# Two batches of 64x64 products on all quarters of the array, softmax denominators inverted by ln and exp on ACT, and other choices of the planner in a two-layer hybrid decoder trunk

## The chip, the core and the metric

The kernel runs on one core of one Trainium2 chip. The core has a matrix engine (PE, which takes weights by separate load instructions, PEld), a vector engine (DVE), an activation engine (ACT), a general engine (POOL), and a queue on SP that issues the DMAs. The metric is the device time of one execution in microseconds (us); lower is better. Beside the timed runs there is one profiled execution, whose records are the trace.

## The reference

Two layers run one after the other on `x` of 512 positions by 1024 channels, float32. Cut to what matters here:

```
for l in range(2):
    h = rmsnorm(x, norm_g[l]);  p = h @ w_in[l]          # one wide projection, split by columns
    o_a = causal latent attention, 8 heads, gated by silu
    o_b = causal attention with a forget gate, 8 heads of 64, gated by silu
    o_c = RWKV-7, 8 heads of 64, gated by silu:
          S_t = S_{t-1} diag(w_t) - (S_{t-1} kk_t)(kk_t a_t)^T + v_t k_t^T ;  y_t = S_t r_t
    merged = sigmoid(g_a)*(o_a @ w_pa) + sigmoid(g_b)*(o_b @ w_pb) + sigmoid(g_c)*(o_c @ w_pc)
    x = x + merged @ w_out
```

Both attentions are softmaxes over 512 keys: `p @ v` is divided by the row sums of `p`. The RWKV recurrence over 512 steps is what the change rewrites most.

## The kernel before, in words

Everything lies transposed: channels on the 128 partitions, the 512 positions along the free dimension. A projection (`proj`, line 776) makes 128 output channels with eight steps over the 1024 inputs, each of three matmuls of 128x128 weights by 512 columns (`mm3`, lines 769 to 772): weights and inputs are split into a high and a low part, and high times high, high times low and low times high are added in one PSUM bank (tag `acc`, three banks). The weights arrive by DMA as float32 (`raw`), 256 columns at a time; `copy` (line 638, on ACT or DVE) makes the high part and `combine` (line 650, on DVE or POOL) the low part, into a ring of six buffers `w`.

The RWKV branch goes by pairs of heads (four pairs in a layer, eight in all); one head lies on partitions 0 to 63, the other on 64 to 127. The 512 steps are cut in 8 chunks of 64. `rwkv_inv` (line 950) makes for each chunk and head a product of 128x128 from 64 rows (line 974, tile names `KB`, `KR`; results in the banks `xk` for the first head, `ch` for the second), masks it into `At`, and inverts a unit triangular matrix: 32x32 blocks on POOL (lines 996, 998), the rest by 32x32 products (lines 1016 and 1022), the inverse in `W`. `rwkv_chain` (line 1027) then makes seven batches of products, each of 16 (8 chunks by 2 heads) and each into the one bank `ch`, by the helper `each` (line 1056): the transposes `KT` as products with the identity (`ch<-cs,KR`), `R` (`ch<-KV,At`), `M` (`ch<-KR,W`), the update of `VSA` (`ch<-At,W`), `Q` (`ch<-At`), `G` (`ch<-KV`, 128 rows by 64) and the transition of the state (`ch<-KV,At` again). All but `G` are 64x64 products in full float32, which the chip runs as two passes each, so a batch of 16 shows as 32 instructions. Both heads of such a batch lie on two quarters of the array, on a diagonal. Each batch needs the batch before it, copied out of PSUM (`copy`). Six steps of the state (lines 1095, 1096) and the output products (lines 1102, 1106) follow.

An attention pair ends in `finish` (line 1230): `dn`, the row sums, is inverted by DVE's reciprocal (line 1232), multiplied by the gate `sg` and then by `ot`. There are 16 of these, one for a pair of heads in each of two attentions and two layers.

The order of the instructions is not the order of the code. Five streams (RWKV preparation, RWKV chain, attention, merge gates, merge) are recorded together, and `plan` (line 214) sets the order on each engine by a list scheduler: of the instructions that could start, the one with the longest way to the end goes first (`urgency`), by a table of costs (`_cost`). For copies, fills and sums it also picks the engine: `elsewhere` (line 349) leaves an instruction to another engine where that one would be done earlier. On PE it may prefer an instruction of the present tile shape (lines 389 to 392), and a change of tile shape costs it a drain (`DRAIN`, lines 426 to 428). A pair of instructions can be tied by hand with `order` (line 580), which puts the one ahead of the other without a wait.

Of the kernel before, what the change touches and what calls it, by code (L numbers as in the profile page):

```python
# [134 lines left out]
PORT_WAIT = 1500  # L135
LN_WAIT = 3000
# [77 lines left out]
def plan(insts, tags, manual, flex, margin, replay=None):  # L214
# [17 lines left out]
    for inst in insts:  # L232
        k = len(ops)
        op = Op(inst, k, box)
        op.cost = _cost(op, psum)
        op.cross = []
        op.array = array(op) if op.kind == "InstMatmult" else None
        op.port = {}
# [15 lines left out]
        op.after.pop(k, None)  # L254
    for a, b in manual:
        ops[index[a]].after[index[b]] = False
# [41 lines left out]
    def forward(follow=None):  # L298
# [13 lines left out]
        mode, pe_end, last_start = (128, 128), 0.0, 0.0  # L312
        other = lambda k: ops[k].func in {"exp": ("Ln",), "ln": ("Exp", "Tanh")}[table]

        def due(k, e):

            return max([ready[k]] + [end[a] + lat(ops[a], ops[k]) for a in ops[k].cross if ops[a].lane != e])

        def ok(k):
            return not wait[k] and not need[k]  # L320

        def release(k):
            if ok(k):
                for e, _ in ops[k].costs:
                    heapq.heappush(later[e], (due(k, e), k))
# [23 lines left out]
        def elsewhere(k, e):  # L349

            mine = starts(k, e) + dict(ops[k].costs)[e]
            for x, cost in ops[k].costs:
                if x != e:
                    ahead = sum(dict(ops[j].costs)[x] for u, j in avail[x]
                                if u < -ops[k].urgency and not taken[j] and len(ops[j].costs) == 1)
                    if max(starts(k, x), free[x] + ahead) + cost < mine:
                        return True
            return False

        def choose():  # L360
# [9 lines left out]
            for s, e in soon:  # L370
# [18 lines left out]
                if e == PE and ops[pick[1]].array != mode:  # L389
# [17 lines left out]
        for _ in ops:  # L407
# [14 lines left out]
            if op.kind == "InstMatmult":  # L422
                c0, c1 = op.outs[0][1:3]
# [107 lines left out]
def build(tc, x_t, wpk, wsm, wv, vec, cst, out, order_of=None, pick={}, queues=None, margin=2.0):  # L531
# [48 lines left out]
    def order(later, earlier):  # L580
        no_sync(later.ins, earlier.ins, "psum bank order")
        manual.append((later.ins.name, earlier.ins.name))

# [132 lines left out]
    for l in range(L):  # L716
# [233 lines left out]
        def rwkv_inv(p, front, v):  # L950
# [3 lines left out]
            KR = rpool.tile([128, 8, 2, 64], F32, name="KR", tag="KR", bufs=2)  # L954
            dve.scalar_tensor_tensor(KR[:, :, 0, :], c64(kn), -1024.0, c64(lw), op0=ALU.mult, op1=ALU.mult)
            combine(KR[:, :, 1, :], c64(r), c64(cum), ALU.mult)
# [45 lines left out]
            for h in range(2):  # L1002
                for b in range(2):
                    o_, l_ = 64 * h + 32 * b, 16 * b + 8 * h
# [5 lines left out]
            half_ = [[slice(o_, o_ + 32) for o_ in (64 * h, 64 * h + 32, SA[h])] for h in range(2)]  # L1010
            for h, (r1, r2, s1) in enumerate(half_):
                fill(W[r2, :, 0:32], 0.0)
                dve.transpose(X[s1], W[r1, :, 0:32])
            for c in range(8):
                for h, (r1, r2, s1) in enumerate(half_):
                    pe.matmul(ps[r2, 0, c, :], At[s1, h, c, 32:64], X[s1, c, :], start=True, stop=True)
            for h, (r1, r2, s1) in enumerate(half_):
                copy(X[r2], ps[r2, 0])
            yield
            for c in range(8):  # L1020
                for h, (r1, r2, s1) in enumerate(half_):
                    pe.matmul(ps[r1, 1, c, :], X[r2, c, :], W[r2, c, 32:64], start=True, stop=True)
            for h, (r1, r2, s1) in enumerate(half_):
# [3 lines left out]
        def rwkv_chain(p, ops):  # L1027
# [19 lines left out]

            R = G = At[:, 0, :, 0:64]
            M = At[:, 1, :, 0:64]
            KT, Q = KR[:, :, 0, :], KR[:, :, 1, :]  # L1050
            chunks = lambda: PS("ch").rearrange("p (c t) -> p c t", t=64)

            def each(ps, out, lhs, rhs):
                for c in range(8):
                    for h, hs in enumerate(HS):
                        pe.matmul(ps[out(h), c, :], lhs(h, c), rhs(h, c), start=True, stop=True)  # L1056

            same, swap = (lambda h: HS[h]), (lambda h: HS[1 - h])
            ps = chunks()
            each(ps, same, lambda h, c: KR[HS[h], c, 0, :], lambda h, c: C["ident"][HS[h], HS[h]])  # L1060
            copy(KT, ps)
            yield
            ps = chunks()
            each(ps, same, lambda h, c: At[HS[h], h, c, 0:64], lambda h, c: VSA[HS[h], c, HS[h]])
            copy(R, ps)
            yield
            ps = chunks()
            each(ps, swap, lambda h, c: W[HS[h], c, :], lambda h, c: KT[HS[h], c, :])
            copy(M, ps)
            yield  # L1070
            ps = chunks()
            each(ps, swap, lambda h, c: W[HS[h], c, :], lambda h, c: R[HS[h], c, :])
            for h, hs in enumerate(HS):
                copy(VSA[HS[1 - h], :, hs], ps[HS[1 - h]])
            yield
            ps = chunks()
            each(ps, same, lambda h, c: M[HS[1 - h], c, :], lambda h, c: At[HS[1 - h], h, c, 64:128])
            dve.tensor_tensor(Q, ps, Q, op=ALU.add)
            yield
            ps = chunks()  # L1080
            each(ps, same, lambda h, c: KBn[:, c, HS[h]], lambda h, c: VSA[:, c, HS[h]])
            dve.tensor_tensor(G, ps, lam.unsqueeze(2).broadcast_to([128, 8, 64]), op=ALU.mult)
            yield
            ps = chunks()
            each(ps, same, lambda h, c: M[HS[1 - h], c, :], lambda h, c: KBn[HS[1 - h], c, HS[h]])
            for h, hs in enumerate(HS):
                fill(KBn[hs, :, HS[1 - h]], 0.0)
                dve.tensor_tensor(KBn[hs, :, hs], ps[hs], C["ident"][hs, hs].unsqueeze(1).broadcast_to([64, 8, 64]),
                                  op=ALU.add)
            yield  # L1090
            Sh = rpool.tile([128, 8, 64], F32, name="Sh", tag="Sh", bufs=1)
            state = [None, G[:, 0, :]] + [Sh[:, c, :] for c in range(2, 8)]
# [137 lines left out]
        def finish(A):  # L1230
            dn, ot = A["dn"], A["ot"]
            dve.reciprocal(dn, dn)  # L1232
# [515 lines left out]
```

## Time and profile before

| | us |
|---|---|
| three timed runs, median (lowest, highest) | 1417.71 (1416.28, 1420.82) |
| the profiled execution, its own time | 1415.31 |
| its span, first to last instruction | 1413.5 |
| PE busy | 1367.5 (97%) |
| PE weight loads busy | 1085.1 (77%) |
| DVE busy | 1171.3 (83%) |
| ACT busy | 777.3 (55%) |
| POOL busy | 452.8 (32%) |

Busy time of an engine is the time in which at least one of its instructions is recorded as running. Matmuls overlap: the record of one goes on while the next has begun, so what a matmul costs PE is read from start to start of two neighbours and not from its duration. The granted clock of PE is 0.995 of its full 2.4 GHz over the whole execution.

### The profile page before, as it was taken

Reading aid. Unit: us, or ns where it says so; the run is one execution under the profiler, and the core shown is the slowest. Engines: PE = TensorE matmul, PEld = TensorE weight load, DVE = VectorE, ACT = ScalarE, POOL = GpSimd, SP = SyncE. Lnnn points to the kernel's source line nnn. Section 1 sums busy time; section 2 is a strip of 40 time slices with the busy share of each in tenths; the row PEclk is TensorE's granted clock in tenths of the full one; section 3 lists DMA queues with packets and bytes.
Section 4 is the critical chain, followed back from the end, with each engine's and each line's share of the span. In section 5 each row is a group of like instructions: output and inputs, shape, how many; then the busy total and the mean of one; then the engine's idle time right before and its main releaser. Section 6 shows DMA issues by size and latency. Waiting matters only on the chain. (4 is left out here: it accounts for less than half of the span.)

```text
span 1413.5 us, 25288 instructions
## 1 busy us (share of the span) xinstructions
PE 1367.5 (97%) x8756; PEld 1085.1 (77%) x8756; DVE 1171.3 (83%) x2653; ACT 777.3 (55%) x1539; POOL 452.8 (32%) x875
## 2 busy tenths in 40 slices
PE   7799999999999999999999999999999999999998
PEld 5676877877778887878877777777876778787787
DVE  8867878888987879878788789789789978898784
ACT  6545637565775466442355656484576664764320
POOL 2152373542650212221002453633724711022210
PEclk9999999999999999999999999999999999999999
DMA  5342322232243234455534342232323233434563
GB/s 170 104 126 75 103 79 87 68 85 81 73 119 95 86 109 159 141 171 169 179 112 139 102 114 82 61 85 84 87 76 116 72 95 90 139 130 156 174 200 97
DMA packets 114625, 158.70 MB, mean 112 GB/s; under 512 B 36544, under 2 KB 44608, under 8 KB 114496
## 3 DMA queue, kind: packets, MB, share of 16 engines
q1 hardware_dynamic: 114496, 157.08, 36.8%
q8 instruction: 69, 1.13, 0.3%
q14 instruction: 60, 0.49, 0.1%
HBM read 128.72 MB, written 28.31 MB: 111 GB/s over the span
## 5 line engine op out<-in xcount | busy, mean ns | idle before, releaser
L770 PE MATMUL acc<-hh,w 128*128 128x512 f32 x1008 | 371.0, 405 | 15.6 <-DVE hh L638 5.1
L650 POOL TENSOR_TENSOR w<-raw,w 128x256 fp32r<-128x256 f32 (+1 forms) x215 | 180.4, 845 | 626.9 <-DVE w L638 292.1
L772 PE MATMUL acc<-hh,w 128*128 128x512 f32 x1008 | 369.8, 404 | 5.3 <-DVE w L650 5.1
L771 PE MATMUL acc<-hl,w 128*128 128x512 f32 x1008 | 366.8, 402 | 1.1 <-DVE hl L650 0.9
L638 ACT ACTIVATE w<-raw 128x256 fp32r<-128x256 f32 (+1 forms) x367 | 147.4, 413 | 247.6 <-PE acc L772 137.9
L770 PEld LDWEIGHTS acc<-hh,w 128*128 128x128 f32 x1008 | 188.7, 190 | 59.9 <-ACT w L638 6.3
L772 PEld LDWEIGHTS acc<-hh,w 128*128 128x128 f32 x1008 | 189.6, 190 | 45.1 <-DVE w L650 5.6
L771 PEld LDWEIGHTS acc<-hl,w 128*128 128x128 f32 x1008 | 189.3, 189 | 41.6 <-DVE hl L650 3.0
L650 DVE TENSOR_TENSOR w<-raw,w 128x256 fp32r<-128x256 f32 x485 | 207.7, 441 | 8.0 <-ACT w L638 3.3
L638 DVE CAST w<-raw 128x256 fp32r<-128x256 f32 (+1 forms) x333 | 98.6, 304 | 98.8 <-PE acc L772 78.6
L996 POOL TENSOR_TENSOR W<-W,NL 128x60 f32<-128x60 f32 (+24 forms) x248 | 88.1, 355 | 72.6 <-DMA NL<-d 55.4
L1204 PE MATMUL wk<-qk 96*128 96x512 f32 (+7 forms) x320 | 99.1, 324 | 1.0 <-ACT vt L638 0.6
L998 POOL TENSOR_TENSOR W<-W 128x60 f32<-128x60 f32 (+24 forms) x248 | 87.9, 354 | 16.9
L650 DVE TENSOR_TENSOR PP<-wk,PP 128x512 fp32r<-128x512 f32 (+3 forms) x128 | 61.4, 485 | 16.5 <-ACT PP L638 14.8
L1204 PEld LDWEIGHTS wk<-qk 128*128 128x128 f32 (+2 forms) x320 | 59.6, 189 | 13.7 <-DVE PP L650 2.1
L1179 DVE CUSTOM_DVE_ANT_0 wk<-wk,cmask 128x128 f32<-128x128 f32 (+3 forms) x128 | 61.3, 497 | 2.5 <-PE wk L1178 1.7
L638 ACT ACTIVATE PP<-wk 128x512 fp32r<-128x512 f32 (+3 forms) x93 | 39.8, 435 | 28.5 <-PE av L1218 24.8
L1232 DVE RECIPROCAL do<-do 128x512 f32<-128x512 f32 x16 | 53.5, 3345 | 0.1
L1205 DVE TENSOR_TENSOR wk<-wk,dmask 128x128 f32<-128x128 f32 x128 | 37.2, 293 | 18.7 <-PE wk L1204 17.9
L1209 ACT ACTIVATE wk<-wk,ncum 128x512 f32<-128x512 f32 (+1 forms) x64 | 31.5, 492 | 27.6 <-DVE wk L1205 27.5
L1178 PE MATMUL wk<-qk 96*128 96x384 f32 (+7 forms) x128 | 42.2, 340 | 2.5 <-DVE ty L1179 2.1
L1216 PE MATMUL av<-PP,Vh 128*128 128x512 f32 (+3 forms) x128 | 42.3, 330 | 0.5 <-ACT do L638 0.2
(529 smaller groups left out, 2894.9 us busy)
## 6 DMA issues: line engine op xcount, KB each, us to landing
raw<-wpk SPq DMA_DIRECT2D x326, 256.0 KB, 2.7
tx<-thd SPq DMA_DIRECT2D x54, 256.0 KB, 3.5
thd<-zth SPq DMA_DIRECT2D x48, 256.0 KB, 2.0
tx<-odr SPq DMA_DIRECT2D x22, 256.0 KB, 3.0
raw<-wpk SPq DMA_DIRECT2D x32, 128.0 KB, 2.4
NL<-d SPq DMA_DIRECT2D x32, 128.0 KB, 2.7
odr<-sg SPq DMA_DIRECT2D x14, 256.0 KB, 2.3
x<-x_t SPq DMA_DIRECT2D x8, 256.0 KB, 4.2
```

What stands on the lines that cost most here:

```text
L638: lambda q: act.activation(dst, src, AF.Copy) if q == ACT else dve.tensor_copy(dst, src))
L650: any_of(costs, lambda q: (dve if q == DVE else gp).tensor_tensor(dst, a, b, op=op))
L770: pe.matmul(ps, wh, xh, start=first, stop=False)
L771: pe.matmul(ps, wh, xl, start=False, stop=False)
L772: pe.matmul(ps, wl, xh, start=False, stop=last)
L996: gp.tensor_tensor(tv, WL[:, 0:m, s:s + 1].broadcast_to([128, m, n]), NL[:, s:s + 1, s + 1:32].broadcast_to([128, m, n]), op=ALU.mult)
L998: gp.tensor_tensor(WL[:, 0:m, s + 1:32], WL[:, 0:m, s + 1:32], tv, op=ALU.add)
L1178: pe.matmul(ps[:, 0:n], t[sr, A["sq"], 128 * i:n], t[sr, 2, 0:n], start=True, stop=True)
L1179: dve.tensor_tensor_reduce(out=ps[:, 0:n], in0=ps[:, 0:n], in1=cmask[:, 512 - n:512], scale=1.0, scalar=NEG, op0=ALU.add, op1=ALU.max, acc ...
L1204: pe.matmul(pv, t[rows, k, js], t[rows, q, q0:512], start=i == 0, stop=i == len(passes) - 1)
L1216: pe.matmul(av[:, q0:512], vh, ph, start=j == 0, stop=False)
L1232: dve.reciprocal(dn, dn)
```

## The change

The diff has five parts.

- `rwkv_chain`: the transposes `KT` become four 128x128 transposes in place of 16 products with the identity, and four copies of 64x256 put them on the other head's partitions. `R` and `M` become one batch of 32 products, in two banks (`ch` and `xk`), and the update of `VSA` and the transition of the state another; in each, the four products of a chunk lie on the four quarters of the array. `Q` and `G` stay batches of 16. For this the inverse `W` lies with the heads exchanged (`SA`), `KR` has its two halves one after the other, and the states go into `KT` in place of a tile of their own.
- `beside` ties the products of a batch one behind the other by `order`, in the two batches and in the product of line 974, where the two heads then alternate.
- The planner starts two batches that are tied together only when both of their banks are free (`mate`), and goes on with a batch that it has begun as long as one of its products can run (`burst`). That holds for every product on a part of the array.
- `PRICE = 400`: where DVE or ACT could take an instruction and POOL could not, DVE is counted as 400 ns later than by its cost.
- `finish`: DVE's reciprocal is replaced by two ACT instructions, ln and exp of minus that.

```diff
+PRICE = 400
...
     for a, b in manual:
-        ops[index[a]].after[index[b]] = False
+        a, b = index[a], index[b]
+        ops[a].after[b] = False
+        if a in firsts and b in firsts:
+            mate[b], mate_of[a], joint[firsts[a]] = a, b, firsts[b]
+    for op in ops:
+        if op.array and op.array != (128, 128):
+            n = op.outs[0][0]
+            op.burst = joint.get(n, n)
...
-            mine = starts(k, e) + dict(ops[k].costs)[e]
+            mine = starts(k, e) + dict(ops[k].costs)[e] + PRICE * (e == DVE and ops[k].costs[0][0] != POOL and ops[k].costs[1][0] != POOL)
...
+                if e == PE and burst:
+                    same = min((x for x in avail[e] if not taken[x[1]] and ops[x[1]].burst == burst), default=None)
+                if same:
+                    pick = same
...
-                for c in range(4 * g, 4 * g + 4):
-                    for h, hs in enumerate(HS):
-                        pe.matmul(two[h][:, c % 4, :], KB0[hs, c].rearrange("p a t -> p (a t)"),
-                                  KR[hs, c].rearrange("p a t -> p (a t)"), start=True, stop=True)
+                beside([pe.matmul(two[h][:, c % 4, :].rearrange("p (a t) -> p a t", a=2),
+                                  KB0[hs, c].rearrange("p a t -> p (a t)"), KR[hs, :, c, :], start=True, stop=True)
+                        for c in range(4 * g, 4 * g + 4) for h, hs in enumerate(HS)])
...
+            for c in range(4):
+                pe.transpose(ps[:, c, :], KT[:, 2 * c:2 * c + 2, :].rearrange("p c t -> p (c t)"), C["ident"])
+            for i, es in enumerate(HS):
+                for h, hs in enumerate(HS):
+                    copy(KT[SH[h], i:8:2, :], ps[es, :, hs])
+            yield
+            pr, pm = chunks(), chunks("xk")
+            beside([one(*a) for c in range(8) for h in range(2) for a in
+                    ((pr[SH[h], c, :], At[HS[h], h, c, 0:64], VSA[HS[h], c, HS[h]]),
+                     (pm[SH[h], c, :], W[SH[h], c, :], KT[SH[h], c, :]))])
+            copy(R, pr)
+            copy(M, pm)
+            yield
+            pu, pt = chunks(), chunks("xk")
+            beside([one(*a) for c in range(8) for h in range(2) for a in
+                    ((pu[SH[h], c, :], W[SH[h], c, :], R[SH[h], c, :]),
+                     (pt[HS[h], c, :], M[SH[h], c, :], KBn[SH[h], c, HS[h]]))])
...
-            dve.reciprocal(dn, dn)
+            act.activation(dn, dn, AF.Ln)
+            act.activation(dn, dn, AF.Exp, scale=-1.0)
```

On PE, the transposes `KT` of the first pair of heads. The tile `cs` holds the identity; before, each 64x64 product of the batch stands between two matmuls of a projection:

```order
L772 MATMUL wk<-w,cqh 128x192
L770 MATMUL acc<-hh,w 128x512
L1056 MATMUL ch<-cs,KR 64x64
L771 MATMUL acc<-hl,w 128x512
L1056 MATMUL ch<-cs,KR 64x64
L772 MATMUL acc<-hh,w 128x512
L1056 MATMUL ch<-cs,KR 64x64
L770 MATMUL acc<-hh,w 128x512
```

and in the changed program the same step has four transposes, of which these are the first two:

```order
L1410 MATMUL wk<-cs,kn__1233 96x128 x4
L1080 MATMUL ch<-cs,KR 128x128
L795 MATMUL acc<-hl,w 128x512
L1080 MATMUL ch<-cs,KR 128x128
L796 MATMUL acc<-hh,w 128x512
```

Transposes of the whole array have taken the place of products on a quarter. Over the program, the 128 products stand in 31 pieces before, and 32 transposes take their place.

On PE again, the batches `R` and `M` of a pair of heads. Before they are two rows of 16 products in the one bank `ch`, with other work between them:

```order
L772 MATMUL wk<-w,cqh 128x192
L1056 MATMUL ch<-KV,At 64x64 x16
L770 MATMUL wk<-w,cqh 128x192
L772 MATMUL wk<-w,ckh 128x256
L771 MATMUL wk<-w,cqh 128x192
L772 MATMUL acc<-hh,w 128x512
L772 MATMUL wk<-w,cqh 128x192
L770 MATMUL acc<-hh,w 128x512
L1056 MATMUL ch<-KR,W 64x64 x16
```

and now one stretch, in which products of the two alternate; these are the last matmul ahead of it and the first five of 32:

```order
L794 MATMUL acc<-hh,w 128x512
L1077 MATMUL ch<-KV,At 64x64
L1077 MATMUL xk<-KR,W 64x64
L1077 MATMUL ch<-KV,At 64x64
L1077 MATMUL xk<-KR,W 64x64
L1077 MATMUL ch<-KV,At 64x64
```

No other matmul stands inside any of the 16 stretches of 32.

Third, the product of line 974 on PE for the second pair of heads (in the changed program line 996). Before, the first head's products (`xk`) and the second's (`ch`) come in groups:

```order
L974 MATMUL xk<-KR,KB_1631 128x128 x3
L974 MATMUL ch<-KR,KB_1631 128x128
L974 MATMUL xk<-KR,KB_1631 128x128
L974 MATMUL ch<-KR,KB_1631 128x128 x3
L770 MATMUL wk<-w,ckh 128x256
```

and now each in turn:

```order
L795 MATMUL acc<-hl,w 128x512
L996 MATMUL xk<-KR,KB_1771 128x128
L996 MATMUL ch<-KR,KB_1771 128x128
L996 MATMUL xk<-KR,KB_1771 128x128
L996 MATMUL ch<-KR,KB_1771 128x128
L996 MATMUL xk<-KR,KB_1771 128x128
```

The eight products are the same; the neighbours now belong to different heads throughout, in 16 stretches of eight where there were 25 stretches.

## Rows read from the trace of the kernel before

**Rows 1.** The page, its busy times: us, share of the span, instructions.

```profile
PE 1367.5 (97%) x8756; PEld 1085.1 (77%) x8756; DVE 1171.3 (83%) x2653; ACT 777.3 (55%) x1539; POOL 452.8 (32%) x875
```

**Rows 2.** Waits, all engines: waiter, releaser, us in total, times, longest.

```profile
ACT w L638 <- PE acc L772: 137.9, 101, 10.7
DVE w L638 <- PE acc L772: 78.6, 86, 3.2
```

**Rows 3.** Waits of PE alone, the longest for ACT.

```profile
PE acc L770 <- ACT w L638: 4.1, 4, 1.6
```

**Rows 4.** Busy times in stretches: PE, PEld, DVE, ACT, POOL; clock; DMA.

```profile
240.00:480.00 240.00, 234.43 (x1907) 187.56 (x1907) 205.71 (x461) 153.63 (x313) 98.68 (x199) 1.00 0.30 88
```

**Rows 5.** Timeline of PE, a whole batch: start, duration, instruction, count.

```profile
231.40 0.40 PE L770 MATMUL acc<-hh,w 128*128 128x512 f32 x1
231.63 0.39 PE L772 MATMUL acc<-hh,w 128*128 128x512 f32 x1
231.95 1.15 PE L1056 MATMUL ch<-cs,KR 64*64 64x64 f32 x32
233.03 0.44 PE L1178 MATMUL wk<-qk 96*128 96x384 f32 x1
```

**Rows 6.** Timeline of PE, batch cut into single products.

```profile
120.02 0.56 PE L1056 MATMUL ch<-cs,KR 64*64 64x64 f32 x10
...
123.49 0.32 PE L1056 MATMUL ch<-cs,KR 64*64 64x64 f32 x2
...
124.17 0.32 PE L1056 MATMUL ch<-cs,KR 64*64 64x64 f32 x2
```

**Rows 7.** Timeline of PE, single transposes between matmuls.

```profile
99.88 0.27 PE L1035 MATMUL ch<-cs,KB 128*128 128x128 f32 x1
...
100.23 0.27 PE L1035 MATMUL ch<-cs,KB 128*128 128x128 f32 x1
```

**Rows 8.** Timeline of PE, batch G on 128 rows by 64 columns.

```profile
177.20 1.15 PE L1056 MATMUL ch<-KV 128*64 128x64 f32 x32
```

**Rows 9.** Timeline of PE, a batch of 32x32 products.

```profile
126.89 0.69 PE L1016 MATMUL xk<-NL,At 32*32 32x32 f32 x32
```

**Rows 10.** Timeline of PE, line 974, a stretch of both heads.

```profile
161.61 0.39 PE L771 MATMUL acc<-hl,w 128*128 128x512 f32 x1
161.93 0.93 PE L974 MATMUL xk<-KR,KB 64*128 64x128 f32 x6
...
163.87 0.38 PE L770 MATMUL wk<-w,ckh 128*128 128x256 f32 x1
```

**Rows 11.** Timeline of PE, line 974, heads in turn; then one head alone.

```profile
166.25 0.27 PE L974 MATMUL xk<-KR,KB 64*128 64x128 f32 x1
166.25 0.27 PE L974 MATMUL ch<-KR,KB 64*128 64x128 f32 x1
166.36 0.27 PE L974 MATMUL xk<-KR,KB 64*128 64x128 f32 x1
...
255.15 1.16 PE L974 MATMUL xk<-KR,KB 64*128 64x128 f32 x8
256.23 0.50 PE L772 MATMUL acc<-hh,w 128*128 128x512 f32 x1
```

**Rows 12.** Groups by line: busy us, mean ns, idle before and its releasers.

```profile
L650 DVE TENSOR_TENSOR w<-raw,w 128x256 fp32r<-128x256 f32 x485 | 207.7, 441 | 8.0 <-ACT w L638 3.3
L638 ACT ACTIVATE w<-raw 128x256 fp32r<-128x256 f32 (+1 forms) x367 | 147.4, 413 | 247.6 <-PE acc L772 137.9 <-issue 34.0 <-PE xk L772 18.0
L638 DVE CAST w<-raw 128x256 fp32r<-128x256 f32 (+1 forms) x333 | 98.6, 304 | 98.8 <-PE acc L772 78.6 <-PE xk L772 5.1 <-issue 4.8
L1232 DVE RECIPROCAL do<-do 128x512 f32<-128x512 f32 x16 | 53.5, 3345 | 0.1
L1411 ACT ACT_TABLE_LOAD x16 | 20.5, 1283 | 0.3
L1412 ACT ACTIVATE ty<-ty 128x512 f32<-128x512 f32 x16 | 10.1, 632 | 0.2
```

More of the change, by code (lines that the diff above doesn't have):

```diff
@@ L237, in plan @@
         op.array = array(op) if op.kind == "InstMatmult" else None
+        op.burst = None
         op.port = {}
@@ L311, in forward @@
         held = [(0.0, 0)] * 5
-        mode, pe_end, last_start = (128, 128), 0.0, 0.0
+        mode, pe_end, last_start, burst = (128, 128), 0.0, 0.0, None
         other = lambda k: ops[k].func in {"exp": ("Ln",), "ln": ("Exp", "Tanh")}[table]
         def due(k, e):
-            return max([ready[k]] + [end[a] + lat(ops[a], ops[k]) for a in ops[k].cross if ops[a].lane != e])
+            t = max([ready[k]] + [end[a] + lat(ops[a], ops[k]) for a in ops[k].cross if ops[a].lane != e])
+            return max(t, ready[mate[k]]) if k in mate else t
         def ok(k):
-            return not wait[k] and not need[k]
+            return not wait[k] and not need[k] and (k not in mate or wait[mate[k]] == 1 and not need[mate[k]])
         def release(k):
+            k = mate_of.get(k, k) if not taken[mate_of.get(k, k)] else k
             if ok(k):
@@ L355, in elsewhere @@
                                 if u < -ops[k].urgency and not taken[j] and len(ops[j].costs) == 1)
-                    if max(starts(k, x), free[x] + ahead) + cost < mine:
+                    if max(starts(k, x), free[x] + ahead) + cost + PRICE * (x == DVE and e == ACT) < mine:
                         return True
@@ L388, in choose @@
                         pick = same
-                if e == PE and ops[pick[1]].array != mode:
+                same = None
+                if e == PE and burst:
+                    same = min((x for x in avail[e] if not taken[x[1]] and ops[x[1]].burst == burst), default=None)
+                if same:
+                    pick = same
+                elif e == PE and ops[pick[1]].array != mode:
                     same = min((x for x in avail[e] if not taken[x[1]] and ops[x[1]].array == mode), default=None)
@@ L582, in order, with beside @@
         manual.append((later.ins.name, earlier.ins.name))
+    def beside(insts):
+        for a, b in zip(insts, insts[1:]):
+            order(b, a)
     cs = cpool.tile([128, NCST], F32, name="cs")
@@ L1049, in rwkv_chain @@
             M = At[:, 1, :, 0:64]
[L1050 to L1058, printed above, removed]
-            ps = chunks()
-            each(ps, same, lambda h, c: KR[HS[h], c, 0, :], lambda h, c: C["ident"][HS[h], HS[h]])
@@ L1061, in rwkv_chain @@
-            copy(KT, ps)
+            KT, Q = KR[:, 0], KR[:, 1]
+            SH = HS[::-1]
+            chunks = lambda tag="ch": PS(tag).rearrange("p (c t) -> p c t", t=64)
+            one = lambda *a: pe.matmul(*a, start=True, stop=True)
+            ps = PS("ch").rearrange("p (c t) -> p c t", t=128)
+            for c in range(4):
[3 more added lines that the diff above has]
+                    copy(KT[SH[h], i:8:2, :], ps[es, :, hs])
@@ new lines, in rwkv_chain @@
+            for h, hs in enumerate(HS):
+                copy(VSA[SH[h], :, hs], pu[SH[h]])
+            ps = chunks()
+            for c in range(8):
+                for hs in HS:
+                    one(ps[hs, c, :], KBn[:, c, hs], VSA[:, c, hs])
+            dve.tensor_tensor(G, ps, lam.unsqueeze(2).broadcast_to([128, 8, 64]), op=ALU.mult)
+            for h, hs in enumerate(HS):
+                fill(KBn[hs, :, SH[h]], 0.0)
+                dve.tensor_tensor(KBn[hs, :, hs], pt[hs], C["ident"][hs, hs].unsqueeze(1).broadcast_to([64, 8, 64]),
+                                  op=ALU.add)
@@ L1062, in rwkv_chain @@
             yield
             ps = chunks()
[L1064 to L1074, printed above, removed]
@@ L1075, in rwkv_chain @@
-            yield
-            ps = chunks()
-            each(ps, same, lambda h, c: M[HS[1 - h], c, :], lambda h, c: At[HS[1 - h], h, c, 64:128])
+            for c in range(8):
+                for h, hs in enumerate(HS):
+                    one(ps[hs, c, :], M[SH[h], c, :], At[SH[h], h, c, 64:128])
             dve.tensor_tensor(Q, ps, Q, op=ALU.add)
             yield
-            ps = chunks()
-            each(ps, same, lambda h, c: KBn[:, c, HS[h]], lambda h, c: VSA[:, c, HS[h]])
-            dve.tensor_tensor(G, ps, lam.unsqueeze(2).broadcast_to([128, 8, 64]), op=ALU.mult)
@@ L1083, in rwkv_chain @@
[L1083 to L1092, printed above, removed]
+            state = [None, G[:, 0, :]] + [KT[:, c, :] for c in range(2, 8)]
```

27 lines of the change are left out of this document (15 added, 12 removed).

## Prediction

> **What bounds the kernel now.** I read the busy times first: PE is busy for 1367.5 us of a span of 1413.5, 97%, and no other engine is over 83% [rows 1]. A busy PE could still be one that trickles, so the waits come next. The engines that split the weights wait for matmuls to end and free their buffers: ACT 137.9 us and DVE 78.6 us, in over eighty waits each [rows 2]. The other way round PE waits little; its longest total on ACT is 4.1 us [rows 3]. So supply runs ahead of PE, and time taken from PE is time taken from the end. Third, in one stretch where RWKV and attention run together PE has 234.4 of 240 us, DVE 205.7, ACT 153.6 [rows 4]: PE is first there too, with DVE 12% behind. A matmul is priced from start to start: a 512-column one takes 231.63 - 231.40 = 0.23 us [rows 5].
>
> **The change, part by part.** All prices are PE time; the sum is made against the profiled execution, 1415.3 us, of which 1413.5 are the span.
>
> A whole batch of 16 products on two quarters costs 233.03 - 231.63 - 0.23 = 1.17 us [rows 5]. That is some 0.93 from its first to its last start and 0.24 for changing the shape of the array in and out. A batch cut up is dearer: a lone product between two matmuls repeats every 124.17 - 123.49 = 0.68 us, so it costs 0.45 beyond the matmul's 0.23 [rows 6].
>
> *Transposes KT.* Of eight batches four are whole (4.7 us), one is cut in 15 and 1 (1.5), and three are cut in 12, 4 and 9 pieces; the starts added up in the same way give 5.2, 2.4 and 4.0. Together 17.8. In their place come 32 transposes of 128x128; one between two matmuls adds (100.23 - 99.88) - 0.23 = 0.12 us [rows 7], 3.8 in all. **-14.0 us.** The copies behind them grow from one to four, on ACT and DVE. I cost that at nothing: PE has projections to run meanwhile. Without that cover it would be some 0.5 us a pair of heads, 4 us.
>
> *Four products in two batches.* Before, 4 x 8 = 32 batches at 1.17 make 37.4 us. After, 16 batches of 32, four quarters in each. What would one cost? The trace has no batch on four quarters, so I bound it. The quarters of a diagonal run side by side: a lone product's record is 0.32 us, five products take 0.56 and sixteen 1.15 [rows 5, 6]. Each pass beyond the first two of the busier quarter adds 0.058 us (0.56 is 0.32 and four of these, 1.15 is 0.32 and fourteen). In the new batch every quarter still has 16 passes, so if the four overlap it is 1.17, with 0.02 more for two further starts; if only two overlap it is 0.93 longer, 2.1. The nearest rows speak for overlap both ways: two column halves that share all rows take the same 1.15 [rows 8], and two row halves that write the same columns of two banks start together, at 166.25 both [rows 11]. Nor do starts seem too dense: 64 in 0.93 is one per 15 ns, and 32x32 passes come 32 in 0.69 us including the last one's own length [rows 9]. I take 1.19: 16 x 1.19 = 19.0. **-18.4 us**; the other end is -3.5.
>
> Here the Trainium skill speaks against the change. TensorEngine Tiling (Array Packing), Gotcha 1, says that row tiles may not use one PSUM bank at the same time; in the new batches both row halves write into `ch`, and both into `xk`. By that rule pairs would take turns, and the batch would be the 2.1 above. The trace before does not agree: the diagonal batches also write one bank from both row halves, and the 1.15 us for 32 passes shows them side by side [rows 5].
>
> *Line 974 in turn.* Where the heads come in groups, PE takes one head's products alone and overlaps few: one such stretch of eight costs 163.87 - 161.61 - 0.23 = 2.03 us [rows 10]. In turn, the two heads start together and the pair moves on every 0.11 us [rows 11]. Sixteen groups, cut in 25 stretches, add up to 32.8 us by their starts. Eight passes of one head alone take 256.23 - 255.15 = 1.08 us with the way out [rows 11], and 0.09 for the way in; sixteen in turn should take that and 0.01, so 16 x 1.18 = 18.9. **-13.9 us.**
>
> *Going on with a batch.* The 32x32 products of line 1022 stand in 14 pieces before and in 8 after; six pieces at about 0.35 (the lone product's 0.45 without its own passes): **-2.1 us.**
>
> *Waiting for two banks.* A joint batch starts only with `ch` and `xk` both free, and everything behind it on PE waits. There are 32 such starts, counting line 974. If each stood for one copy of the bank it needs, 0.6 us, that is 19 us; below nothing it cannot go, since a batch that waits for one bank alone waits no longer. The planner has projections to put ahead, so I take nothing and keep the 19 for the range.
>
> *Other engines.* DVE loses 16 reciprocals, 53.5 us [rows 12]. By the two orders, copies of 256 columns go from 355 to 195 on DVE and from 441 to 633 on ACT, and low parts from 211 to 98 on POOL and from 513 to 626 on DVE. At 304, 413 and 441 ns [rows 12] that is -49 and +50 on DVE and +79 on ACT; 53 copies of 512 columns off DVE make some -25 there and +33 on ACT. ACT also gets 32 ln and exp at 0.63, 20 us, and 30 more table loads (97 to 127) at 1.283, 38 us [rows 12]. So DVE goes to some 1090 us and ACT to some 950 of 1370: 80% and 70%, both still behind PE. These hide behind PE as the weights do now. If the cover is gone, what is late is ACT: it is one queue, and a score's exp stands behind a table load and an ln for 1.9 us.
>
> Sum: 14.0 + 18.4 + 13.9 + 2.1 = 48.4, so 1366.9. PE stood still for 46 us before (span less busy), much of it short waits; a PE that is 3.5% faster meets its suppliers a little more often. I add 2 for that. The median of the runs is 2.4 above the profiled execution, which gives 1371.3. **Forecast 1371 us**, 3.3% faster; by the spread of stalls 1360 to 1382.
>
> **Rivals.**
>
> *Four quarters don't overlap.* Then 16 x 0.93 = 15 us stay: 1386. For it: no row shows four at once, and the rule on banks above. Against: both halves of the claim are in rows 8 and 11. TensorE: Matmul & The Clock Gate, Part 1, gives some 25 ns as the least distance between starts, which would make a batch of 64 passes 1.6 us and the time 1382; the 32x32 rows, under 22 ns, do not agree [rows 9].
>
> *The gain is given back to supply.* PE needs its weights 3.5% sooner, DVE is the next engine [rows 4], and joint batches hold two banks. If 20 of the 48.4 come back as waits for `w` or `xk`: 1391. Against it: suppliers wait for PE now, by 216 us [rows 2], and DVE is relieved.
>
> *ACT's queue decides, and the kernel is slower.* Sixteen finishes put 28 table loads (by the order) with a ln or exp behind each into ACT's queue, 1.9 us apiece, with scores and weights behind them. If each holds PE for its full length, 28 x 1.9 = 53 us, more than the 48.4 gained: 1424. It decides from 1.7 us per load on. For it: ACT serves the scores in order. Against: 97 loads stand in the queue now, and PE's waits for ACT are a few us [rows 3].
>
> *PE's waits shrink as well.* DVE no longer stands 3.3 us in a reciprocal 16 times, and its pairs with POOL are fewer. If 18 of the 46 us go too: 1353.
>
> **Chances.** Forecast 0.62, quarters that don't overlap 0.13, gain given back 0.12, shrinking waits 0.08, ACT's queue 0.05. The range of 1352 to 1396 takes in the first four and leaves out the last and the worse part of the third. A measurement here tells a difference of about 0.3% (4 us) from none. All cases but ACT's queue are faster by more; 0.03 of given back and ACT's queue together may end within that: faster 0.92, same 0.03, slower 0.05.
>
> **What the changed profile would show.** Transposes: 32 rows at line 1080 and no cut batches. Quarters: the joint batches as 64 instructions in about 1.17 us; about 2.1 would prove them serial. Line 974 (now 996): stretches of 16 passes from first to last start in 0.89 us. PE busy near 1320 us, its idle time still near 46; DVE near 1090, ACT near 950. Wrong would be: PE idle over 65 us, with waits for ACT at the scores, `w` or the exp of the finishes, or for `xk` at the head of joint batches.

## The result, and the profile after

The changed kernel takes 1399.3 us (median of four runs, 1398.75 to 1401.48) where the kernel before, beside it, took 1417.1 (1416.28 to 1420.82). The ratio is 0.9872 with an interval of 0.9851 to 0.9893: 1.3% faster. The forecast was 1371 and the range ended at 1396, so the direction was right and less than half of the gain came. The profiled execution took 1399.46 us, 1397.7 of them the span.

The busy times of the page answer to [rows 1] (busy us, share of the span, instructions):

```profile
PE 1333.1 (95%) x8532; PEld 1051.7 (75%) x8532; DVE 1078.8 (77%) x2488; ACT 943.4 (67%) x1900; POOL 362.5 (26%) x749
```

DVE and ACT came out as worked out (1090 and 950). PE did not: it is busy for 13 us more than the 1320 forecast, and it stands still for 1397.7 - 1333.1 = 64.6 us, where 46 before and some 48 were forecast. Both show, in good part, in the same places. These are busy times in stretches of 20 us at the end of each layer's RWKV (columns as in [rows 4]: stretch, length, PE, PEld, DVE, ACT, POOL, granted clock, DMA share, GB/s):

```profile
540.00:560.00 20.00, 20.00 (x147) 16.55 (x146) 14.62 (x47) 14.03 (x31) 3.71 (x4) 1.00 0.27 80
560.00:580.00 20.00, 13.38 (x51) 9.84 (x49) 10.99 (x26) 13.62 (x25) 1.05 (x2) 0.73 0.24 73
580.00:600.00 20.00, 16.30 (x55) 11.90 (x56) 11.04 (x20) 7.64 (x15) 1.43 (x1) 0.76 0.65 204
1270.00:1290.00 20.00, 12.03 (x38) 8.88 (x39) 11.21 (x22) 10.27 (x19) 0.00 (x0) 0.66 0.46 159
```

In the kernel before, the same stretch of the first layer was full:

```profile
560.00:580.00 20.00, 20.00 (x94) 15.94 (x93) 16.39 (x46) 10.96 (x22) 1.68 (x3) 1.00 0.35 112
```

PE runs dry there, and no other engine is full: what is left is a chain. The timeline of PE after shows what ends it (start, duration, instruction, count; in brackets the idle time before and its releaser):

```profile
576.15 0.31 PE L1239 MATMUL av<-PP,Vl 128*64 128x128 f32 x1
577.52 0.47 PE L1240 MATMUL av<-PP,Vh 128*128 128x128 f32 x1 [1.06 <-DVE PP L674]
583.68 0.79 PE L794 MATMUL ch<-mT,w 128*128 128x512 f32 x1 [5.69 <-ACT mT L662]
...
585.51 0.63 PE L794 MATMUL ch<-mT,w 128*128 128x512 f32 x1
585.94 0.63 PE L795 MATMUL ch<-mKR,w 128*128 128x512 f32 x1
```

The 5.69 us are spent on `mT`, the high part of RWKV's output, which is the input of the product `o_c @ w_pc` in the merge. RWKV's last output is stored by 580.28, when DVE makes one part of `mT`. The parts that ACT makes come later, behind the table loads, the ln and the exp of a `finish` (lines 1254 and 1255):

```profile
580.28 0.43 DVE L662 CAST mT<-tx 128x512 fp32r<-128x512 f32 x1 [0.38 <-DMA odr<-KV]
579.24 1.28 ACT L1254 ACT_TABLE_LOAD   x1
580.53 0.63 ACT L1254 ACTIVATE do<-do 128x512 f32<-128x512 f32 x1
581.18 1.28 ACT L1255 ACT_TABLE_LOAD   x1
582.48 0.63 ACT L1255 ACTIVATE do<-do 128x512 f32<-128x512 f32 x1
583.01 1.65 ACT L662 ACTIVATE mT<-tx 128x512 fp32r<-128x512 f32 x3
```

So up to 2.7 us of this wait (580.28 to 583.01) can be ACT's queue; the rest is the late end of RWKV. And after it two neighbours of 512 columns start 0.43 us apart, where 0.23 is the rule [rows 5]: PE runs at the lower of its two clocks, 1.2 of 2.4 GHz. The granted clock is 0.50 in these two stretches, one in each layer:

```profile
569.20:589.70 20.50, 12.32 (x31) 8.69 (x32) 12.47 (x24) 13.60 (x21) 2.48 (x3) 0.50 0.39 129
1272.40:1286.00 13.60, 6.73 (x16) 4.93 (x16) 7.16 (x13) 7.18 (x11) 0.00 (x0) 0.50 0.55 193
```

By waits (in total, times, longest), PE's largest one is now that for `mT`, once in each layer; the longest for ACT was 4.1 before [rows 3]:

```profile
PE ch L794 <- ACT mT L662: 11.4, 2, 5.7
PE acc L794 <- DVE hh L662: 5.4, 1, 5.4
```

Why is the end of RWKV late? The timeline of PE in the changed kernel, around the first batch `R` and `M` of the first pair of heads:

```profile
216.48 0.69 PE L1039 MATMUL xk<-NL,At 32*32 32x32 f32 x32
...
218.47 0.69 PE L1045 MATMUL xk<-W,NL 32*32 32x32 f32 x32
...
222.12 0.40 PE L928 MATMUL xk<-WA,tx 128*128 128x512 f32 x1
...
228.90 0.40 PE L690 MATMUL xk<-PP,bd 128*128 128x512 f32 x1
...
229.48 0.39 PE L691 MATMUL xk<-PP,bd 128*128 128x512 f32 x1
...
230.62 0.39 PE L794 MATMUL acc<-hh,w 128*128 128x512 f32 x1
230.94 0.27 PE L1077 MATMUL ch<-KV,At 64*64 64x64 f32 x1
230.95 0.27 PE L1077 MATMUL xk<-KR,W 64*64 64x64 f32 x1
...
231.88 0.22 PE L1077 MATMUL xk<-KR,W 64*64 64x64 f32 x1
232.03 0.42 PE L1410 MATMUL wk<-cs,kn__2245 128*96 128x128 f32 x2
```

In the kernel before, the first pair's `R` started at 167.64 us:

```profile
167.64 0.56 PE L1056 MATMUL ch<-KV,At 64*64 64x64 f32 x12
```

Now its transposes end at 148, its next batch stands in `xk` behind the *second* pair's inversion (lines 1039 and 1045) and the first products of the *third* pair's preparation (lines 928, 690 and 691, in `xk` as well), and starts at 230.94. The second pair's two joint batches lie 78 us apart, at 286.1 and 363.7, with the third pair's inversion between them in `xk`. The steps of the state (line 1117, 1095 before) of the eight pairs start at 243, 374, 438, 539 and 960, 1101, 1182, 1250 us, before at 184, 278, 360, 483 and 903, 1003, 1100, 1183. The first step of each pair, after and before (line, count, ns, first and last start):

```profile
L1117 PE MATMUL ch<-At,KV x16: 217/275/295, 243.0 to 1250.2; 128*128 128x64 f32 x16
L1095 PE MATMUL ch<-At,KV x16: 217/275/294, 183.9 to 1183.2; 128*128 128x64 f32 x16
```

The attentions start where they did (first scores at 139 against 145) and are through earlier: the last scores of the two layers start at 544 and 1249 us, where it was 597 and 1300. So the projections and attentions that should cover the chain are used up when it is still running. The scores before (the line of the changed kernel stands in experiment 1):

```profile
L1178 PE MATMUL wk<-qk x128: 220/337/504, 144.9 to 1299.6; 96*128 96x128 f32 x16, 96*128 96x256 f32 x16, 96*128 96x384 f32 x16, 96*128 96x512 f32 x16
```

The same rows say that the price of a joint batch was right: 64 passes from 230.94 to 231.88, and 0.15 to the next start.

### The profile page after: what moved, and what is told of

Its sections match the earlier page's. It is cut to its first block, busy times and chain, and to the rows that moved or that the text cites. A ratio compares the mean times of both kernels' runs of the same rounds, so it can differ in the third digit from the quotient of the medians.

```text
span 1397.7 us, 25030 instructions
## 1 busy us (share of the span) xinstructions
PE 1333.1 (95%) x8532; PEld 1051.7 (75%) x8532; DVE 1078.8 (77%) x2488; ACT 943.4 (67%) x1900; POOL 362.5 (26%) x749
## 5 line engine op out<-in xcount | busy, mean ns | idle before, releaser
L662 ACT ACTIVATE w<-raw 128x256 fp32r<-128x256 f32 (+1 forms) x521 | 208.2, 412 | 254.7 <-PE acc L796 145.3
L674 DVE TENSOR_TENSOR w<-raw,w 128x256 fp32r<-128x256 f32 (+1 forms) x598 | 251.2, 434 | 81.4 <-ACT w L662 75.0
L674 POOL TENSOR_TENSOR w<-raw,w 128x256 fp32r<-128x256 f32 (+1 forms) x102 | 92.8, 915 | 395.3 <-ACT w L662 199.7
L1226 PE MATMUL wk<-qk 96*128 96x512 f32 (+11 forms) x320 | 93.7, 326 | 2.0 <-DVE PP L674 1.4
L662 DVE CAST w<-raw 128x256 fp32r<-128x256 f32 (+1 forms) x179 | 53.4, 306 | 48.3 <-PE acc L796 42.2
L1226 PEld LDWEIGHTS wk<-qk 96*128 96x128 f32 (+2 forms) x320 | 59.8, 191 | 18.1 <-DVE PP L674 8.2
L662 ACT ACTIVATE PP<-wk 128x512 fp32r<-128x512 f32 (+3 forms) x120 | 50.9, 432 | 7.8 <-PE av L1240 3.6
L1238 PE MATMUL av<-PP,Vh 128*128 128x512 f32 (+3 forms) x128 | 43.6, 340 | 3.3 <-DVE PP L662 2.0
L1231 ACT ACTIVATE wk<-wk 128x512 f32<-128x512 f32 (+1 forms) x64 | 26.8, 423 | 28.7 <-DVE wk L1227 28.2
L1240 PE MATMUL av<-PP,Vh 128*128 128x512 f32 (+3 forms) x128 | 43.7, 342 | 1.3 <-DVE PP L674 1.3
```

Of the source, the lines that this page charges most:

```text
L662: lambda q: act.activation(dst, src, AF.Copy) if q == ACT else dve.tensor_copy(dst, src))
L674: any_of(costs, lambda q: (dve if q == DVE else gp).tensor_tensor(dst, a, b, op=op))
L1226: pe.matmul(pv, t[rows, k, js], t[rows, q, q0:512], start=i == 0, stop=i == len(passes) - 1)
L1238: pe.matmul(av[:, q0:512], vh, ph, start=j == 0, stop=False)
L1240: pe.matmul(av[:, q0:512], vh, pl, start=False, stop=j == 3)
```

## The experiments

All times are medians beside the kernel before on the same chip; a ratio is to that kernel, with its interval.

**1. The second bank of the joint batches in `wk`.** The kernel has two banks `wk`, which the attention scores use, and one each of `xk` and `ch`.

```diff
-            pr, pm = chunks(), chunks("xk")
+            pr, pm = chunks(), chunks("wk")
-            pu, pt = chunks(), chunks("xk")
+            pu, pt = chunks(), chunks("wk")
```

> Edit: the second bank of both joint batches is taken from the two banks wk of the attention, not from the one bank xk that the RWKV preparation uses. Theory (the bank xk, given out in recorded order, holds a pair's joint batches back until the next pair's inversion has ended; the RWKV chains end late and PE runs dry before the merge): the chains move forward, PE's idle time goes from 65 to under 46 us, both stretches at half clock go, and the time is 1399 - 28 = 1371 us (1362 to 1380). Rival A (ACT's longer queue delays everything): unchanged, 1395 to 1403. Rival B (a joint batch must find two banks free at once, whichever they are): unchanged or slower, 1395 to 1410.

Measured: 1555.7 us, 1.0966 (1.0938 to 1.0995). A miss, by far. All RWKV chains are early (state steps at 165 to 377 us), and the attentions late. These are the scores' instructions (line 1200: count, shortest, median and longest ns, first and last start), in this kernel and then in the changed one:

```profile
L1200 PE MATMUL wk<-qk x128: 220/385/797, 396.9 to 1460.9; 96*128 96x128 f32 x16, 96*128 96x256 f32 x16, 96*128 96x384 f32 x16, 96*128 96x512 f32 x16
```

```profile
L1200 PE MATMUL wk<-qk x128: 220/336/505, 138.6 to 1248.7; 96*128 96x128 f32 x16, 96*128 96x256 f32 x16, 96*128 96x384 f32 x16, 96*128 96x512 f32 x16
```

The first layer's scores now come behind all four chains of RWKV. Whoever shares banks with a chain is queued with it, because banks of a name are handed out in the order in which the streams were recorded. It went the other way round, but it is the same mechanism: two streams that ran past each other now stand in line. PE pays: this is a stretch of the second layer in this kernel, with 48 of 200 us idle and the clock at 0.78:

```profile
1000.00:1200.00 200.00, 151.94 (x1416) 116.15 (x1415) 111.72 (x241) 102.09 (x201) 56.85 (x148) 0.78 0.20 53
```

**2. The inversion's last products in `wk`**, the joint batches left in `xk`.

```diff
-            ps = PS("xk").rearrange("p (i c t) -> p i c t", i=2, t=32)
+            ps = PS("wk").rearrange("p (i c t) -> p i c t", i=2, t=32)
```

> Edit: the joint batches stay in ch and xk; instead the last 32x32 products of the inversion (lines 1039 and 1045 of the changed kernel) use a bank wk. Theory: it breaks the same tie at its other end, so 1371 us (1362 to 1382) with the chains early. Rival A (ACT's queue): unchanged, 1395 to 1403. Rival B (two banks at once): unchanged, 1395 to 1403.

Measured: 1556.4 us, 1.0989 (1.0950 to 1.1029). A miss with the same picture: chains at 160 to 395 us, first scores at 419.

**3. Four batches apart.** `R`, `M`, the update and the transition again as four batches of 16, each in `ch` alone; the rest as changed. There are two runs; the second is on the same chip as the second run of experiment 6.

```diff
-            pr, pm = chunks(), chunks("xk")
-            beside([one(*a) for c in range(8) for h in range(2) for a in
-                    ((pr[SH[h], c, :], At[HS[h], h, c, 0:64], VSA[HS[h], c, HS[h]]),
-                     (pm[SH[h], c, :], W[SH[h], c, :], KT[SH[h], c, :]))])
-            copy(R, pr)
-            copy(M, pm)
+            ps = chunks()
+            for c in range(8):
+                for h in range(2):
+                    one(ps[SH[h], c, :], At[HS[h], h, c, 0:64], VSA[HS[h], c, HS[h]])
+            copy(R, ps)
...
```

> Edit: R, M, the update of VSA and the transition are four batches of 16 in ch again, as in the kernel before; all else as in the changed kernel (transposes, alternating heads, ln and exp, PRICE). Theory: PE has 32 batches at 1.17 in place of 16 at 1.19 us, 18 more, but the tie is gone and so are some 28 us of idle time: 1399 + 18 - 28 = 1389 (1380 to 1396), so not slower than the joint version. Rival A (ACT) and rival C (the idle time has nothing to do with the joint batches): 1399 + 18 = 1417.

> The kernel with four batches of 16 in ch once more, beside the next kernel on one chip and in five rounds, so that the two can be set against each other: what joining the batches is worth when no bank is in the way. Theory (PE's work sets the time, so that the 18 us which joining takes from PE come out of the end): this kernel 1380 to 1384, the joined one 1362 to 1366. Rival (the earlier single looks, 1381.7 against 1376.2, hold: part of what PE is relieved of comes back as idle time of PE, 40 us here and 53 there): this kernel 1380 to 1384, the joined one 5 to 10 us below.

Measured: 1381.7 us, 0.9749 (0.9724 to 0.9773), and 1381.8, 0.9759 (0.9744 to 0.9775). The theory held, by more than it asked. Without the joint batches the kernel is 17.6 us faster than with them, though PE has more to do. Its busy times (second run, span 1381.7):

```profile
PE 1340.2 (97%) x8532; PEld 1071.2 (78%) x8532; DVE 1075.0 (78%) x2439; ACT 949.0 (69%) x1916; POOL 388.0 (28%) x782
```

PE is idle for 41.5 us, less than before the change, and the state steps start at 193 to 446 and 903 to 1159. So the late chains come with the joint batches, and with nothing else in the change.

**4. Without the part for ACT**: the changed kernel with DVE's reciprocal and no price on DVE.

```diff
-PRICE = 400
+PRICE = 0
...
-            act.activation(dn, dn, AF.Ln)
-            act.activation(dn, dn, AF.Exp, scale=-1.0)
+            dve.reciprocal(dn, dn)
```

> Edit: the changed kernel with DVE's reciprocal back and PRICE at 0; joint batches in ch and xk stay. Theory: the chains stay late and PE runs dry as in the changed kernel, 1399 (1392 to 1408), with DVE at about 1170 us busy and ACT about 780. Rival A (ACT's longer queue took the gain): it comes back, 1371 (1362 to 1380).

Measured: 1409.5 us, 0.9933 (0.9910 to 0.9956), state steps at 245 to 546 and 958 to 1261. ACT is idle nearly half of the time here, and the chains are as late as in the changed kernel: the rival that blames ACT's queue is refuted. The part for ACT is worth 10 us in this kernel.

**5. The tie in the order loosened, in `xk`.** The planner makes a first pass from which the order of recording is taken. Here the second bank of a joint batch has a name of its own in that pass, as the banks `acc` had already; in the real pass it is `xk` as before.

```diff
-        if dry and tag == "acc":
-            b, tag = DRY["acc"], tag + z
+        if dry and z:
+            b, tag = 1, tag + z
...
-            pr, pm = chunks(), chunks("xk")
+            pr, pm = chunks(), chunks("xk", "c")
-            pu, pt = chunks(), chunks("xk")
+            pu, pt = chunks(), chunks("xk", "c")
```

> Edit: joint batches in ch and xk as in the changed kernel; only in the planner's first pass, the one whose recorded order is arbitrary, they get a bank of their own, so that the order in which xk is handed out comes from the planned times. Two runs before this one moved a joint bank to wk and came out at 1555 us with attention held until RWKV had ended (first score matmul at 397 us, 139 in the changed kernel). Theory (the recorded order in which a shared bank is handed out ties streams of work to each other, whichever bank it is): with that order planned, neither RWKV nor attention is late, PE idle is under 46 us, no stretch at half clock, 1382 (batches apart) less 18 for the joint batches = 1364 us (1358 to 1380). Rival B (the joint batch itself, waiting for two banks, is what costs): about the changed kernel's 1399.

Measured: 1405.1 us, 0.9913 (0.9894 to 0.9932); the theory missed. The chains of the first two pairs come early in both layers (180, 271; 881, 982), but the third still stands behind the fourth pair's inversion. The timeline of PE in this kernel:

```profile
1114.62 0.39 PE L796 MATMUL acc<-hh,w 128*128 128x512 f32 x1
1124.44 0.28 PE L1039 MATMUL xk<-NL,At 32*32 32x32 f32 x2 [9.43 <-issue]
...
1127.00 1.15 PE L1045 MATMUL xk<-W,NL 32*32 32x32 f32 x32 [0.95 <-issue]
1128.08 0.47 PE L1077 MATMUL ch<-KV,At 64*64 64x64 f32 x2
```

PE stands 9.43 us in front of line 1039, whose inputs come from POOL's inversion and its DMAs, and the third pair's joint batch follows at once when that is through. The planned order of PE's instructions has the batch behind line 1039: a bank that both use puts the batch behind a wait that is not its own.

**6. The same with `wk`.**

```diff
-            pr, pm = chunks(), chunks("xk", "c")
+            pr, pm = chunks(), chunks("wk", "c")
-            pu, pt = chunks(), chunks("xk", "c")
+            pu, pt = chunks(), chunks("wk", "c")
```

> Edit: as the run at 1555 us (second joint bank in wk), but with a bank of its own in the planner's first pass. Theory (recorded order): the 1555 goes away altogether, 1358 to 1385, near the run with xk. Rival (wk is a bad bank for it because attention needs both its buffers): stays over 1450.

> The kernel with the joint batches in ch and wk, with a bank of their own in the planner's first pass, once more and on the same chip as the kernel with the batches apart. Theory: 18 us below that one, 1362 to 1366. Rival: 5 to 10 us below it, 1372 to 1378, with PE idle for some 53 us of its span against some 40.

Measured: 1376.2 us, 0.9707 (0.9686 to 0.9728), and again 1375.9, 0.9716 (0.9700 to 0.9731). It is the fastest of all, and beats both kernels. A joint batch needs two free banks at once here too, so the rival that blames this alone is refuted. State steps start at 184 to 453 and 880 to 1165 us, and the first joint batch where `R` was before (line 1077, count, ns, first and last start, in this kernel's second run):

```profile
L1077 PE MATMUL ch<-KV,At x32: 218/218/267, 169.9 to 170.8; 64*64 64x64 f32 x32
L1077 PE MATMUL wk<-KR,W x32: 218/218/267, 169.9 to 170.8; 64*64 64x64 f32 x32
```

Its busy times, of a span of 1375.2:

```profile
PE 1322.3 (96%) x8532; PEld 1051.5 (76%) x8532; DVE 1075.6 (78%) x2437; ACT 933.4 (68%) x1897; POOL 393.8 (29%) x799
```

PE's busy time is the one forecast (some 1320). Against the batches apart, on the same chip, PE has 17.9 us less to do, yet the time falls by 5.9: PE's idle time grows from 41.5 to 52.9 us. The larger part of that lies where RWKV and attention run. The two stretches, first with the batches apart and then in this kernel:

```profile
150.00:450.00 300.00, 290.89 (x2435) 233.40 (x2434) 240.33 (x556) 216.13 (x437) 111.45 (x252) 0.99 0.30 88
850.00:1150.00 300.00, 291.63 (x2333) 228.83 (x2333) 241.09 (x537) 220.59 (x449) 128.20 (x261) 0.99 0.31 90
```

```profile
150.00:450.00 300.00, 287.76 (x2438) 230.78 (x2438) 238.98 (x552) 214.30 (x452) 117.89 (x261) 0.99 0.31 89
850.00:1150.00 300.00, 285.92 (x2223) 223.17 (x2222) 244.79 (x556) 214.20 (x432) 125.45 (x270) 0.99 0.31 91
```

17.5 us idle of 600 become 26.3. So the rival of the last pair of expectations holds: a third of what joining takes from PE comes out at the end.

**7. Batches apart, without the part for ACT**: experiments 3 and 4 together, so the transposes, line 996 in turn and going on with a batch, alone.

```diff
+            ps = chunks()
+            for c in range(8):
+                for h in range(2):
+                    one(ps[SH[h], c, :], At[HS[h], h, c, 0:64], VSA[HS[h], c, HS[h]])
...
+            dve.reciprocal(dn, dn)
```

> Edit: batches apart, and DVE's reciprocal and PRICE 0 as before; what is left of the change are transposes, heads in turn and going on with a batch. By the prices of the prediction: 14.0 + 13.9 + 2.1 = 30 us off 1417, 1387; if the ACT part is worth as much here as in the joint kernel (1409.5 against 1399.3, 10 us) this is 1382 + 10 = 1392. If the ACT part is worth nothing where PE does not run dry: 1382.

Measured: 1383.9 us, 0.9761 (0.9743 to 0.9779). PE is busy for 1337.3 us of 1382.0. That is 30.2 less than before, by three terms whose sum was 30.0. Beside experiment 3 the part for ACT is worth 2 us here, which is less than the two intervals can tell from nothing.

**8. The part for ACT alone**, on the kernel before.

```diff
+PRICE = 400
...
-            dve.reciprocal(dn, dn)
+            act.activation(dn, dn, AF.Ln)
+            act.activation(dn, dn, AF.Exp, scale=-1.0)
```

> Edit: the kernel before with ln and exp in place of the reciprocal and PRICE 400 alone. If the ACT part is worth what it is worth in the joint kernel: 1417 - 10 = 1407 us. Theory of the prediction (hidden behind PE on either engine): 1417 (1412 to 1419). Rival A (ACT's queue hurts): over 1420.

Measured: 1405.3 us, 0.9909 (0.9887 to 0.9931). PE's busy time hardly changes (1366.1 of a span of 1403.2), but it stands still for 37 us in place of 46.

**9. A second user of `xk` loosened**: experiment 5, with the two banks of the heads' product (line 996) under names of their own in the first pass too. The other products of the preparation that use `xk` (lines 690, 691, 928, 1039 and 1045 among them) stay tied.

```diff
-                two = [PS(tag).rearrange("p (c t) -> p c t", t=128) for tag in ("xk", "ch")]
+                two = [PS(tag, "i").rearrange("p (c t) -> p c t", t=128) for tag in ("xk", "ch")]
```

> The joint batches stay in ch and xk, and in the planner's first pass both they and the two banks of the heads' product (line 996) have banks of their own, so that the recorded order ties neither to the other. In the order of PE's instructions the chain of a layer's third pair then stands ahead of the fourth pair's last inversion products in the first layer (1911 against 2382 of its instructions) but not in the second (5558 against 5542), where the kernel with the batches alone untied (1405) had it behind in both layers. Theory (the order in which the bank xk is handed out is what costs): the dry spell of the first layer goes, that of the second stays, and the time lies half way between 1405 and the 1376 of the version in wk, 1385 to 1395, with PE busy again at 430 to 440 us and still standing at 1115 to 1165. Rival (one bank xk for two users costs by itself, however it is ordered): 1400 to 1410, with PE waits at the joint batches or at line 1039 in both layers.

Measured: 1464.7 us, 1.0331 (1.0299 to 1.0364), above what either theory gave. In the second layer PE stood in front of line 1039 for much longer, with the third pair's chain right behind it:

```profile
1110.68 0.39 PE L796 MATMUL acc<-hh,w 128*128 128x512 f32 x1
1133.70 0.28 PE L1039 MATMUL xk<-NL,At 32*32 32x32 f32 x2 [22.63 <-issue]
...
1136.34 1.07 PE L1045 MATMUL xk<-W,NL 32*32 32x32 f32 x32 [0.96 <-issue]
1137.33 0.47 PE L1077 MATMUL ch<-KV,At 64*64 64x64 f32 x2
```

That wait is the mechanism of experiment 5 once more. It does not make up the whole loss, and the rest of it was not followed up.

**10. The kernel of experiment 6 without the part for ACT** (the edit is that of experiment 4).

> The best version so far (joint batches in ch and wk, untied in the first pass; 1376) with the ACT part of the change taken out: DVE's reciprocal, and no price on DVE. Theory (PE is the bound there, 96% busy, and both engines behind it have room, so relieving DVE is worth no more than the 2 us that it was worth beside batches apart): 1374 to 1380. Rival (relieving DVE pays as it did in the changed kernel and in the kernel before, 10 to 12 us): 1385 to 1390.

Measured: 1382.8 us, 0.9754 (0.9718 to 0.9790), 6.6 above experiment 6's first run. It lies between the two expectations, and with an interval of some 5 us to each side it decides for neither.

## Why the prediction was wrong, step by step

**The step that failed** is "Waiting for two banks": "The planner has projections to put ahead, so I take nothing and keep the 19 for the range." The size was wrong, and so was the thing priced. I priced a batch that waits for one copy of a bank, some 0.6 us at a time. What happened is that `xk` joined the RWKV chain to the preparation of the pairs behind it, which until then ran past it. The first pair's `R` and `M` come 63 us later than `R` came before, where 0.6 was priced, and PE has projections to put ahead meanwhile, as I said; they are then missing at the end of the layer. Against the profiled forecast of 1368.9 (1366.9 and 2 of stalls) the execution is 30.6 us longer. Of these, 1333.1 - (1367.5 - 48.4) = 14.0 are PE busy for longer and 64.6 - 48 = 16.6 are PE idle. PE's 8532 instructions are the same in number with the batches in `wk`, and take 1322.3 there.

Shown: without the joint batches the 17.6 us come back (experiment 3), with them in `wk` and untied 23 (experiment 6), and without the part for ACT the chains are as late and nothing comes back (experiment 4). The other bank alone (experiment 1) or the loosened order alone (experiment 5) does not help; the two together do. Seen in the traces, not isolated: which products ahead in `xk` hold the batches up, line 1039 and its input above all. How much of the loss is the order of recording and how much that there is only one bank `xk`, where `wk` has two, stays open: experiments 5 and 9 loosened the order alone, and only for some users of `xk`, and did not help.

**Transposes, line 974 in turn, going on with a batch.** Right in their sum: -14.0, -13.9 and -2.1 make 30.0, and PE lost 30.2 (experiment 7); no run has one of them alone. Line 996 in turn is shown best by one stretch, whose first pair, last pair and next start answer to [rows 10, 11]:

```profile
74.38 0.37 PE L996 MATMUL xk<-KR,KB 64*128 64x128 f32 x1
74.38 0.37 PE L996 MATMUL ch<-KR,KB 64*128 64x128 f32 x1
...
75.26 0.27 PE L996 MATMUL xk<-KR,KB 64*128 64x128 f32 x1
75.27 0.27 PE L996 MATMUL ch<-KR,KB 64*128 64x128 f32 x1
75.47 0.50 PE L794 MATMUL acc<-hh,w 128*128 128x512 f32 x1
```

That is the 0.89 us foreseen; 13 of the 16 stretches have it.

**Four products in two batches.** As PE time right: -18.4 foreseen, 17.9 between experiments 3 and 6. As time at the end worth 5.9 with the bank out of the way, since PE, the less it has to do there, waits the more.

**Other engines.** Their busy times were right, but not the price of nothing. The 54 us of reciprocals and the copies taken from DVE are worth 12 us by themselves (experiment 8), 10 in the changed kernel, and beside the batches apart no more than the runs can tell (2). Alone it took 9 us from PE's idle time (46 to 37), and hardly any from its work.

**The rivals.** Quarters that don't overlap: refuted by 0.94 us for 64 passes. Gain given back: nearest by its number (1391), and `xk` was the place, but I had given it a chance of 0.12 and bounded it by 20 us; and no wait of a joint batch for `xk` stands among PE's waits, since PE did other work until it had none. PE's waits shrink: true at half its size for the part for ACT alone (9 of 18 us, experiment 8), while the whole change left PE idle for longer. ACT's queue decides: refuted by experiment 4, in which the kernel is slower without ACT's part; what the trace has of it are the up to 2.7 us ahead of `mT`.

## What to carry to other kernels

Before two operations are joined, ask who else uses each buffer of the joint one, and in which order they take turns: a buffer shared by two chains that used to pass each other is a dependency of the length of a chain, not of a copy. Where work runs in order, compare when each chain *starts and ends* in the two orders, not only what an engine has to do in sum; one that ends 50 us later meets an engine that has nothing left to cover it. And a relief of 18 us on an engine that is 97% busy may be worth a third of that.

## What the runs showed of the hardware that was not expected

Four quarters of the array cost 0.943 us from first to last start for 64 passes of 64x64, where two quarters took 0.930 for 32 (the batches `Q` of the same execution). That is one start per 15 ns, and each of the two banks is written from both row halves in that time, to different partitions.

Idle time of PE showed twice here. Among gaps of 0.8 to 5.7 us at the end of each layer the granted clock of 20 us was 0.73, 0.76 and 0.66, and neighbours of 512 columns started 0.43 us apart in place of 0.23, so that the busy time went up too. An estimate from these rows: PE was busy for 12.32 and 6.73 us at the lower clock, and by 0.23 to 0.43 some 9 of these 19 us would not have been there at the higher one. The kernel before has some time at the lower clock too (0.995 granted over the whole, 0.985 now), so this is only a part of the 14.0 us by which PE was busy for longer; the rest was not followed up. The Trainium skill (TensorE: Matmul & The Clock Gate, "Wait — 56ns, not 53.3ns?") gives 426.7 ns for that distance at the lower clock and 215.7 at the higher; the first agrees with the trace, and the second is 0.23 here.
